# A two-pass list schedule: TensorE's order from a first pass, the other engines ordered by deadlines in a second

## The chip, the core and the metric

The kernel runs on one core of a Trainium2 chip. The metric is the time on the device of one execution, in microseconds (us), as the median of several. The core has five engines with a queue of instructions each: TensorE (PE, the matmuls, with its weight loads shown apart as PEld), VectorE (DVE), ScalarE (ACT), GpSimd (POOL) and SyncE (SP), which here issues the DMA transfers.

## The reference

A trunk of two layers on x of 1024 tokens by 1024 features, all float32. Layer 0 mixes tokens with a gated MLP, layer 1 with an HGRN2 recurrence; each is followed by a gated convolutional feed-forward network. The shifts, scales and gates (`mod`) come from a vector c through a matrix of 1024 by 6144 for each layer.

```python
cond = jax.nn.silu(c)
for i in range(DEPTH):
    mod = (cond @ ada_w[i] + ada_b[i])[:, None, :]
    sh1, sc1, g1, sh2, sc2, g2 = jnp.split(mod, 6, axis=-1)
    h = rms_norm(x, norm_g[i, 0]) * (1.0 + sc1) + sh1
    if i % N_MIXERS == 0:
        y = spatial_gating_mixer(h, ...)   # (gelu(h @ w_u) * (ws @ layernorm(gelu(h @ w_v)) + b)) @ w_out
    else:
        y = hgrn2_mixer(h, ...)            # q, f, i, g = h @ w_in; gated recurrence in chunks of 64; @ w_out
    x = x + g1 * y
    h = rms_norm(x, norm_g[i, 1]) * (1.0 + sc2) + sh2
    x = x + g2 * conv_ffn(h, ...)          # (gelu(conv3(h @ w_gate)) * conv3(h @ w_val)) @ w_down
return rms_norm(x, final_g)
```

## The kernel before

Every float32 matmul is made of three: both operands are split into a high piece (ACT, a copy in a shorter format) and a low piece (the rest, a subtraction on DVE or POOL), and `mm3` (L247) multiplies high by high, high by low and low by high. `p_split` (L442 to L448) makes the two pieces of a weight or of a sum, `p_h` (L428 to L433) those of a normalized activation. Most large products go by a Strassen scheme: a pair of weight blocks gives seven products of sums of quarters. `p_comb` (L455) and `shifted` (L621) make the sums, `snap` (L673, ACT) and `add` (L676, DVE) bring the products out of PSUM.

The stages follow one another in time, by the profile's clock: the start (x arrives, its mean square, first modulations); the v half of the gated MLP, whose result goes to DRAM (`vd`); the u half with the spatial mix (L1194) of v, which is loaded again (L1163) and normalized on ACT (`norm`, L1171), and gated on DVE (`done`, L1210), about 230 to 400 us; the out-projection (`block_out`), 400 to 543, which loads weights (`in_wo`) and gated activations (`gact`) from DRAM; the feed-forward up-projection with its convolution (`conv` L831, `finish` L813), 543 to 1000, and down-projection, to 1220; the HGRN2 scan, to 1710; its out-projection, to 1800; the second feed-forward network, to 2440; and the final norm (`diag` L313, `bcast` L318 on PE, `p_final` L1667).

The modulations are dot products on DVE: `p_ada` loads 512 KB of the matrix (`in_ada`) and `p_dot` or `first_values` multiplies and sums it (`ada_dot`, L255). Those of layer 1 are spread as filler over the stages of layer 0.

What sets the order: the code does not issue instructions as it is written. `Plan.op` records an operation (one or a few instructions) with its engine, a stated duration, what it reads and writes, and a priority `pr` written by hand. `emit` (L162) then runs a list schedule over all operations: on every step it takes, among those that are ready, the one that could start earliest by the stated durations, and among equals the one with the lowest `pr`. Operations of DVE and POOL with `port=True` are never put at the same time. The result is one fixed order for each engine and for SP's queue of DMA issues; the engines then run in that order, each waiting by semaphores for what it needs.

Of the kernel before, what the change touches and what calls it, by code (L numbers as in the profile page):

```python
# [98 lines left out]

class Plan:  # L100
# [9 lines left out]
    LOAD = 2.0  # L110

# [50 lines left out]
    def emit(self):  # L162
        n = len(self.ops)
        left = [0] * n
        users = [[] for _ in range(n)]
        for i, o in enumerate(self.ops):
            for q in set(o[3]):
                users[q].append(i)
                left[i] += 1
# [7 lines left out]
        while len(order) < n:  # L177
            best = None
            for eng, lst in ready.items():
                f = free.get(eng, 0.0)  # L180
                for i in lst:
                    o = self.ops[i]
                    t = max(f, est[i], port if o[5] else 0.0)
                    if best is None or (t, o[4], i) < best:
                        best = (t, o[4], i)
            t, _, i = best
            eng, dur, fn, _, _, pt = self.ops[i]
# [26 lines left out]
def trunk(tc, a, pool, psum, dram):  # L214
# [168 lines left out]
    def p_evac(pl, ps, d, hs, gate, which, pr):  # L383
# [23 lines left out]
    def p_stats(pl, nm, accv, ps, rbv, pr, part=0):  # L407
# [8 lines left out]
        pl.op("V", 1.3, chain, r=(ps,), w=(sm,), pr=pr)  # L416
# [25 lines left out]
    def p_split(pl, src, hi, lo, eng, pr, *preds):  # L442
# [4 lines left out]
        return pl.op(eng, (0.1 + 0.53 * w) if eng == "V" else 0.1 + 1.17 * w,  # L447
# [131 lines left out]
    class Pairs:  # L579
# [32 lines left out]
        def combos(self, k, pr, t1=None):  # L612
# [7 lines left out]
            def shifted(out, x, s, y, srg, pr):  # L620
                pl.op("V", 0.67, lambda: V.scalar_tensor_tensor(out=out.f, in0=x.f, scalar=s, in1=y.f,  # L621
# [26 lines left out]
        def pair(self, j, fine=False):  # L648
# [26 lines left out]
            def add(c, ps, i):  # L675
                pl.op("V", 0.75, lambda: V.tensor_tensor(out=c.f, in0=ps.f, in1=c.f, op=ALU.add), r=(ps, c),  # L676
# [1112 lines left out]
```

## Time and profile before

| | |
|---|---|
| median of 3 runs | 2470.67 us (2470.39 to 2472.54) |
| the profiled execution | 2468.28 us, of which the span of the core's instructions is 2466.5 us |
| TensorE busy | 2419.2 us, 98% of the span |
| VectorE, ScalarE, GpSimd busy | 1992.3, 1205.9, 487.2 us |
| mean granted TensorE clock | 0.993 of full speed |

The span runs from the first to the last instruction; the 1.8 us between it and the execution's time lie around it. A busy share is an average over stages with different limits: a stage is read by its own windows.

### The profile page before, as it was taken

What the parts mean: (1) busy time and instruction counts of PE and PEld (TensorE: products, weight loads), DVE (VectorE), ACT (ScalarE), POOL (GpSimd) and SP (SyncE); (2) the same over time, 40 slices, a digit from 0 to 9 for tenths busy, and PEclk for the clock granted to TensorE, in tenths of its full rate; (3) what the DMA queues carried; (4) which work ended last, traced back from release to release, by engine and by line L of the source; (5) the groups of instructions that cost most, each with busy time, mean ns of one, the idle gap of its engine ahead of it and who ended that gap; (6) DMA issues with size and microseconds to landing.
All of it is one profiled execution on the core that took longest, in us unless ns stands there. A gap on an engine that the chain in (4) does not pass through costs nothing.

```text
span 2466.5 us, 33569 instructions
## 1 busy us (share of the span) xinstructions
PE 2419.2 (98%) x11850; PEld 2024.6 (82%) x11850; DVE 1992.3 (81%) x3179; ACT 1205.9 (49%) x2067; POOL 487.2 (20%) x294
## 2 busy tenths in 40 slices
PE   9999999999999999999999999999999999999997
PEld 7878777788788888888899898888777888888886
DVE  8989987988998888967746666658998998889766
ACT  5324654455555554445544444435454555554544
POOL 0232211122222221013321111100312222220122
PEclk9999999999999999999999999999999999999998
DMA  9997678621333324734110111123302332238332
GB/s 356 305 344 272 200 238 295 222 77 39 116 102 108 116 94 143 262 112 120 51 48 35 58 42 56 44 73 106 106 24 95 98 132 99 94 127 283 95 116 81
DMA packets 156411, 332.00 MB, mean 135 GB/s; under 512 B 15825, under 2 KB 34641, under 8 KB 156242
## 3 DMA queue, kind: packets, MB, share of 16 engines
q1 hardware_dynamic: 156242, 329.86, 40.0%
q8 instruction: 93, 1.52, 0.3%
q14 instruction: 76, 0.62, 0.1%
HBM read 254.82 MB, written 74.97 MB: 134 GB/s over the span
## 4 chain that ended last, share of the span: by engine, by line
PE 76%; DVE 8%; DMA 3%; ACT 2%; issue 1%; SPq 0%; DVEq 0%; ACTq 0%
PE pb L247 69%; PE pb L1462 3%; DMA n<-in_wo 1%; DMA xT<-vd 1%; DMA n<-in_down 1%; DVE h L448 1%; ACT xT L1171 1%; PE pb L1531 1%; PE pb L1551 1%; DVE w L448 1%; DVE raw L831 1%; PE pb L1553 1%; DVE n L448 0%; DVE xT L455 0%; DVE w L455 0%
## 5 line engine op out<-in xcount | busy, mean ns | idle before, releaser
L247 PE MATMUL pb<-h,w 128*128 128x512 f32 (+1 forms) x4212 | 981.7, 389 | 12.8 <-DVE h L448 4.1
L247 PE MATMUL pb<-n,w 128*128 128x512 f32 x3936 | 951.6, 394 | 6.8 <-ACT wk L673 4.4
L247 PEld LDWEIGHTS pb<-h,w 128*128 128x128 f32 x4212 | 785.5, 188 | 185.0 <-DVE h L448 9.6
L247 PEld LDWEIGHTS pb<-n,w 128*128 128x128 f32 x3936 | 731.9, 188 | 160.0 <-ACT wk L673 5.5
L448 POOL TENSOR_TENSOR w<-w,w 128x512 fp32r<-128x512 f32 x158 | 252.2, 1604 | 862.5 <-ACT w L445 784.2
L445 ACT ACTIVATE w<-w 128x512 fp32r<-128x512 f32 x384 | 237.3, 626 | 212.4 <-PE pb L247 121.7
L247 PE MATMUL pb<-w,n 128*128 128x512 f32 (+1 forms) x1536 | 273.6, 338 | 3.0 <-POOL w L448 1.7
L247 PEld LDWEIGHTS pb<-w,n 128*128 128x128 f32 x1536 | 237.9, 190 | 36.3 <-POOL w L448 2.1
L831 DVE SCALAR_TENSOR_TENSOR raw<-wk,prm,raw 128x1024 f32<-128x1024 f32 x168 | 251.7, 1520 | 16.2 <-ACT raw L827 14.1
L448 POOL TENSOR_TENSOR w<-raw,w 128x1024 fp32r<-128x1024 f32 (+1 forms) x48 | 118.3, 2473 | 536.0 <-ACT w L445 467.0
L448 DVE TENSOR_TENSOR w<-w,w 128x512 fp32r<-128x512 f32 x226 | 166.4, 741 | 41.5 <-ACT w L445 41.4
L673 ACT ACTIVATE wk<-pb 128x512 f32<-128x512 f32 x160 | 95.2, 599 | 174.5 <-PE pb L247 161.9
L445 ACT ACTIVATE w<-n 128x512 fp32r<-128x512 f32 x136 | 85.7, 630 | 158.0 <-PE pb L247 143.7
L676 DVE TENSOR_TENSOR wk<-pb,wk 128x512 f32<-128x512 f32 x160 | 109.2, 687 | 50.1 <-PE pb L247 30.9
L448 DVE TENSOR_TENSOR w<-n,w 128x512 fp32r<-128x512 f32 x136 | 103.4, 763 | 56.5 <-ACT w L445 56.4
L445 ACT ACTIVATE h<-h 128x512 fp32r<-128x512 f32 x198 | 122.3, 619 | 40.8 <-DMA h<-gact 23.5
L827 ACT ACTIVATE raw<-wk,prm 128x1024 f32<-128x1024 f32 x84 | 104.2, 1243 | 41.6 <-DVE wk L676 34.9
L448 POOL TENSOR_TENSOR h<-h,h 128x512 fp32r<-128x512 f32 x48 | 67.8, 1413 | 258.8 <-ACT h L445 247.4
L1468 DVE TENSOR_TENSOR wk<-wk 128x256 f32<-128x256 f32 x192 | 95.6, 523 | 23.7 <-PE pb L1462 11.0
L255 DVE SCALAR_TENSOR_TENSOR h<-h,raw 128x1024 f32<-128x1024 f32 x81 | 111.1, 1404 | 3.5 <-DMA h<-in_ada 3.4
L448 DVE TENSOR_TENSOR h<-h,h 128x512 fp32r<-128x512 f32 x150 | 102.1, 686 | 8.7 <-ACT h L445 8.7
L1472 ACT ACTIVATE wk<-wk 128x256 f32<-128x256 f32 x192 | 73.9, 415 | 59.4 <-PE pb L1462 44.2
(217 smaller groups left out, 2431.8 us busy)
## 6 DMA issues: line engine op xcount, KB each, us to landing
w<-in_up SPq DMA_DIRECT2D x88, 512.0 KB, 3.5
h<-in_ada SPq DMA_DIRECT2D x81, 512.0 KB, 6.3
act<-raw SPq DMA_DIRECT2D x154, 256.0 KB, 2.0
h<-act SPq DMA_DIRECT2D x124, 256.0 KB, 2.7
n<-in_down SPq DMA_DIRECT2D x64, 256.0 KB, 5.3
h<-gact SPq DMA_DIRECT2D x56, 256.0 KB, 2.7
gact<-xT SPq DMA_DIRECT2D x52, 256.0 KB, 3.9
vd<-h SPq DMA_DIRECT2D x32, 256.0 KB, 5.1
```

The lines of the kernel that those rows point to most:

```text
L247: PE.matmul(ps, L[i // 2], R[i % 2], start=first and i == 0 and not more, stop=last and i == 2, skip_group_check=more)
L255: V.scalar_tensor_tensor(out=raw, in0=raw, scalar=1.0, in1=condr, op0=ALU.mult, op1=ALU.mult, accum_out=mod[:, m:m + 1])
L445: pl.op("S", 0.2 + 0.43 * w, lambda: S.activation(hi.r, src.f, AF.Copy), r=(src,), w=(hi,), pr=pr)
L448: lambda: e.tensor_tensor(out=lo.r, in0=src.f, in1=hi.f, op=ALU.subtract), *preds,
L673: pl.op("S", 0.6, lambda: S.activation(c.f, ps.f, AF.Copy), r=(ps,), w=(c,), pr=p(i) - 10)
L676: pl.op("V", 0.75, lambda: V.tensor_tensor(out=c.f, in0=ps.f, in1=c.f, op=ALU.add), r=(ps, c), w=(c,), pr=p(i) - 8)
L827: pl.op("S", 1.15, lambda: S.activation(y.f, wk[:, o + PADW:o + PADW + T], AF.Identity, bias=pc("conv_b", l * NUP + b), scale=cw(2)), r=(c ...
L831: pl.op("V", 1.17, lambda w=w: V.scalar_tensor_tensor(out=y.f, in0=wk[:, o + w:o + w + T], scalar=cw(w), in1=y.f, op0=ALU.mult, op1=ALU.ad ...
L1171: S.activation(x, x, AF.Identity, scale=lnr[:, tb:tb + 1], bias=nmr[:, tb:tb + 1])
L1462: PE.matmul(ps_()[0:m, c, :], K.f[:, c * P:c * P + m], q, start=True, stop=True)
L1468: V.tensor_tensor(out=halves_(X2, s)[:, :, i, :], in0=halves_(X, s)[:, :, i, :], in1=pair2()[:, :, o].unsqueeze(2).to_broadcast([P, 256 // ...
L1472: S.activation(halves_(X2, s)[:, :, i, :], halves_(X, s)[:, :, i, :], AF.Copy)
```

## The change

`emit` schedules twice. The first pass is the old schedule by hand priorities. From it comes PE's order. Each PE operation then gets as its due time the sum of the stated durations of the PE operations ahead of it; an operation of another engine gets the earliest due time of what uses its result, less its own stated duration and a lag, and one whose result nothing on PE uses gets the end of the plan. The second pass is the same list schedule (earliest start first), with PE's operations ranked by their place in the first order and the others by due time, in place of `pr`. Beside that the stated durations of some operations are set to what was measured. No instruction is added, taken away or altered; the orders on the engines and the order of SP's DMA issues differ.

```diff
-    def emit(self):
+    def lag(self, i, u):
+        eng, e2 = self.ops[i][0], self.ops[u][0]
+        return self.LOAD if eng == "D" else self.LAT if e2 != eng else self.CHAIN if eng == "V" else 0.0
+
+    def schedule(self, users, rank):
...
                 for i in lst:
-                    o = self.ops[i]
-                    t = max(f, est[i], port if o[5] else 0.0)
-                    if best is None or (t, o[4], i) < best:
-                        best = (t, o[4], i)
+                    t = max(f, est[i], port if self.ops[i][5] else 0.0)
+                    if best is None or (t, rank[i], i) < best:
+                        best = (t, rank[i], i)
...
+    def emit(self):
...
+        order = self.schedule(users, [o[4] for o in self.ops])
+        for _ in range(self.ROUNDS):
+            on_pe = [i for i in order if self.ops[i][0] == "PE"]
+            late, t = [FAR] * n, 0.0
+            for i in on_pe:
+                late[i] = t
+                t += self.ops[i][1]
+            for i in reversed(order):
+                for u in users[i]:
+                    late[i] = min(late[i], late[u] - self.lag(i, u) - self.ops[i][1])
+            rank = [min(x, t) for x in late]
+            for k, i in enumerate(on_pe):
+                rank[i] = k
+            order = self.schedule(users, rank)
+        for i in order:
             self.ops[i][2]()
...
-        pl.op("V", 1.3, chain, r=(ps,), w=(sm,), pr=pr)
+        pl.op("V", 1.95, chain, r=(ps,), w=(sm,), pr=pr)
...
-        return pl.op(eng, (0.1 + 0.53 * w) if eng == "V" else 0.1 + 1.17 * w,
+        return pl.op(eng, (0.11 + 0.57 * w) if eng == "V" else 0.1 + 1.22 * w,
...
-                    pl.op("S", 1.2, norm, r=(v, kv(3280 + 4 * hf, 4), kv(3544 + 4 * hf, 4)), w=(v,), pr=pr - 3)
+                    pl.op("S", 1.6, norm, r=(v, kv(3280 + 4 * hf, 4), kv(3544 + 4 * hf, 4)), w=(v,), pr=pr - 3)
```

Three places in the orders. A row is the line, the operation, and out<-in by the program's names; lines of the changed kernel stand 25 higher from `trunk_body` on (L255 is L280 there, L433 L458, L448 L473, L459 L484).

**DVE at the start**, about 19 to 27 us: the row at L433 (L458), `n100`, is the low piece of the first activation block; the five rows from L255 to L970 (L280 to L995) behind or ahead of it are `first_values` of the second block, and `w1`, `w3` are low pieces of weights. Before:

```order
L448 TENSOR_TENSOR w1_196<-h2_133,w0_167 128x1024
L448 TENSOR_TENSOR w3_202<-h3_145,w2_176 128x1024
L433 SCALAR_TENSOR_TENSOR n100_207<-h11_186,mod_70,n000_200 128x512
L255 SCALAR_TENSOR_TENSOR h4_162,mod_70<-h4_162,raw2_67 128x1024
L255 SCALAR_TENSOR_TENSOR h5_172,mod_70<-h5_172,raw2_67 128x1024
L263 TENSOR_TENSOR mod_70<-mod_70,prm_63 128x2
L267 SCALAR_TENSOR_TENSOR amul_71<-mod_70,prm_63 128x1
L970 SCALAR_TENSOR_TENSOR h11_186<-xT_64,amul_71,h10_198 128x512
L448 TENSOR_TENSOR w5_244<-h6_179,w4_205 128x1024
```

And of the change:

```order
L995 SCALAR_TENSOR_TENSOR h11_186<-xT_64,amul_71,pb6_81 128x512
L473 TENSOR_TENSOR w3_198<-h3_132,w2_164 128x1024
L473 TENSOR_TENSOR w1_203<-h2_140,w0_174 128x1024
L280 SCALAR_TENSOR_TENSOR h4_160,mod_70<-h4_160,raw2_67 128x1024
L280 SCALAR_TENSOR_TENSOR h5_170,mod_70<-h5_170,raw2_67 128x1024
L288 TENSOR_TENSOR mod_70<-mod_70,prm_63 128x2
L292 SCALAR_TENSOR_TENSOR amul_71<-mod_70,prm_63 128x1
L995 SCALAR_TENSOR_TENSOR h11_186<-xT_64,amul_71,h10_205 128x512
L458 SCALAR_TENSOR_TENSOR n100_207<-h11_186,mod_70,n000_201 128x512
```

The low piece `n100` went from ahead of the second block's five rows to behind them.

**SP's queue of DMA issues**, where the gated MLP's out-projection loads stand (`n...<-in_wo` are weights, `h11` and `h2<-gact` activations, `in_ada` modulations of layer 1, `gact<-xT` stores). Before:

```order
L459 DMA n021_2973<-in_wo 128x512
L459 DMA h11_2988<-gact_84 128x512
L459 DMA h2_2993<-gact_84 128x512
L459 DMA n031_2996<-in_wo 128x512
L459 DMA raw1_66<-in_ada 128x1024
L739 DMA gact_84<-xT_64 128x512
L459 DMA h11_2988<-gact_84 128x512
L459 DMA h2_2993<-gact_84 128x512
L459 DMA h11_2988<-gact_84 128x512
L459 DMA h10_3038<-in_ada 128x1024
L459 DMA n101_3051<-in_wo 128x512
L739 DMA gact_84<-xT_64 128x512 x4
```

And of the change:

```order
L484 DMA n021_2972<-in_wo 128x512
L484 DMA h11_2988<-gact_84 128x512
L484 DMA h2_2993<-gact_84 128x512
L484 DMA n031_2997<-in_wo 128x512
L484 DMA n101_3000<-in_wo 128x512
L484 DMA h11_2988<-gact_84 128x512
L484 DMA h2_2993<-gact_84 128x512
L484 DMA n111_3025<-in_wo 128x512
L484 DMA n121_3029<-in_wo 128x512
L484 DMA h11_2988<-gact_84 128x512
L484 DMA n131_3046<-in_wo 128x512
L484 DMA h2_2993<-gact_84 128x512
```

Two loads of modulations stood here among those of the out-projection; in the change its next loads have their places. From the load of `n001` to that of `n071` eight stood in the queue before, and none stands there in the change.

**DVE ahead of the HGRN2 out-projection's fifth product**, about 1731 to 1738 us: `n041`, `n141` and so on are the low pieces for it (L448, L473), `raw2`, `h0`, `h9` and `n020` to `n130` are sums for later (L455, L480), `xT` an evacuation (L387, L412). Before:

```order
L1575 SCALAR_TENSOR_TENSOR h9_9709<-pb2_77,prm_63,h6_8816 128x512
L455 TENSOR_TENSOR n120_12939<-n060_12844,n020_12841 128x512
L455 TENSOR_TENSOR raw2_67<-h9_9709,raw2_67 128x512
L455 TENSOR_TENSOR h0_9273<-h9_9709,h0_9273 128x512
L455 TENSOR_TENSOR h9_9709<-h9_9709,raw2_67 128x512
L455 TENSOR_TENSOR n030_12882<-w8_12158,n030_12882 128x512
L448 TENSOR_TENSOR n041_12712<-n100_12833,n001_12650 128x512
L387 SCALAR_TENSOR_TENSOR xT_64<-pb0_75,mod_70,xT_64 128x512
L387 SCALAR_TENSOR_TENSOR xT_64<-pb1_76,mod_70,xT_64 128x512
L455 TENSOR_TENSOR n130_12979<-n070_12888,n030_12882 128x512
L448 TENSOR_TENSOR n141_12769<-w1_12161,n101_12669 128x512
```

And of the change:

```order
L1600 SCALAR_TENSOR_TENSOR h9_9710<-pb2_77,prm_63,h6_8845 128x512
L473 TENSOR_TENSOR n041_12675<-n100_12894,n001_12633 128x512
L473 TENSOR_TENSOR n141_12682<-w1_12158,n101_12635 128x512
L480 TENSOR_TENSOR raw2_67<-h9_9710,raw2_67 128x512
L473 TENSOR_TENSOR n051_12751<-n110_12896,n011_12644 128x512
L473 TENSOR_TENSOR n151_12793<-w1_12158,n111_12648 128x512
L480 TENSOR_TENSOR n020_12790<-w8_12160,n020_12790 128x512
L473 TENSOR_TENSOR n161_12842<-w5_12211,n121_12663 128x512
```

The low pieces `n041` and `n141` come right behind `h9`, ahead of the sums that stood in front of them.

## Rows read from the trace of the kernel before

**Rows 1.** The profile page: busy time of the engines (us, share of the span, instructions).

```profile
PE 2419.2 (98%) x11850; PEld 2024.6 (82%) x11850; DVE 1992.3 (81%) x3179; ACT 1205.9 (49%) x2067; POOL 487.2 (20%) x294
```

**Rows 2.** Windows by stage: us of the stretch, busy us (and instructions) of PE, PEld, DVE, ACT, POOL, then TensorE's granted clock as a share of full speed, the DMA share and GB/s.

```profile
100.00:200.00 100.00, 98.33 (x430) 80.06 (x429) 89.48 (x142) 27.36 (x43) 35.56 (x14) 1.00 0.91 322
...
620.00:700.00 80.00, 78.84 (x344) 64.44 (x345) 76.66 (x87) 42.68 (x61) 22.23 (x12) 1.00 0.33 112
700.00:900.00 200.00, 200.00 (x884) 165.67 (x883) 178.38 (x209) 103.76 (x148) 43.32 (x31) 1.00 0.32 110
...
1220.00:1700.00 480.00, 479.06 (x3157) 429.58 (x3156) 295.48 (x744) 207.76 (x442) 71.41 (x32) 1.00 0.15 50
```

**Rows 3.** Finer windows, same columns.

```profile
260.00:280.00 20.00, 16.87 (x77) 13.86 (x76) 20.00 (x31) 14.88 (x34) 6.83 (x2) 0.91 0.58 191
...
400.00:420.00 20.00, 17.63 (x69) 13.59 (x68) 13.90 (x22) 8.72 (x15) 1.29 (x1) 0.91 0.98 342
420.00:440.00 20.00, 18.07 (x79) 14.26 (x78) 16.95 (x28) 7.75 (x13) 0.00 (x0) 1.00 0.94 333
440.00:460.00 20.00, 18.99 (x82) 14.77 (x81) 18.46 (x32) 10.49 (x19) 0.00 (x0) 1.00 0.94 336
...
1840.00:1860.00 20.00, 18.38 (x75) 13.50 (x74) 19.84 (x28) 10.88 (x19) 5.08 (x3) 1.00 0.04 14
1860.00:1880.00 20.00, 16.22 (x62) 12.87 (x61) 15.10 (x14) 9.27 (x14) 5.67 (x4) 0.86 0.27 92
```

**Rows 4.** What PE waited for over the whole span, from the chain of waits: us in total, times, longest us.

```profile
PE pb L318 <- DVE h L313: 7.7, 6, 4.9
PE pb L247 <- ACT xT L673: 4.6, 4, 1.6
...
PE pb L247 <- POOL w L448: 1.7, 1, 1.7
```

**Rows 5.** Timeline of PE and of DVE at the start: start us, us, engine, line, operation, out<-in, count; in brackets the idle time before it and what ended it.

```profile
21.39 5.75 PE L247 MATMUL pb<-w,n 128*128 128x512 f32 x24 [0.93 <-ACT n L432]
27.31 0.98 PE L247 MATMUL pb<-w,n 128*128 128x512 f32 x3 [0.17 <-ACT n L432]
...
22.28 0.75 DVE L433 SCALAR_TENSOR_TENSOR n<-h,mod,n 128x512 fp32r<-128x512 f32 x1
22.94 1.22 DVE L255 SCALAR_TENSOR_TENSOR h<-h,raw 128x1024 f32<-128x1024 f32 x1
...
25.75 0.75 DVE L970 SCALAR_TENSOR_TENSOR h<-xT,amul,h 128x512 f32<-128x512 f32 x1
```

**Rows 6.** Timeline of PE and of ACT in the u half: the spatial mix that waits, and a product whose bank ACT frees.

```profile
263.01 1.74 PE L1194 MATMUL pb<-wk,xT 128*128 128x128 f32 x8 [2.43 <-ACT h L445]
...
369.35 0.96 PE L247 MATMUL pb<-h,w 128*128 128x512 f32 x3 [1.57 <-ACT xT L673]
...
367.17 1.65 ACT L1171 ACTIVATE xT<-xT,wk 128x128 f32<-128x128 f32 x4 [0.32 <-DMA xT<-vd]
368.72 0.57 ACT L673 ACTIVATE xT<-pb 128x512 f32<-128x512 f32 x1
```

**Rows 7.** Issues of loads from 366 to 441 us by L459: count, then the issuing instruction's own ns min/median/max, first and last start; and PE's waits in that stretch.

```profile
L459 SPq DMA_DIRECT2D h<-in_ada x6: 327/327/463, 403.6 to 440.7; - x6
L459 SPq DMA_DIRECT2D raw<-in_ada x5: 328/333/377, 366.7 to 419.4; - x5
...
402.53 0.50 PE L247 MATMUL pb<-h,w 128*128 128x512 f32 x1 [2.06 <-ACT h L445]
...
432.02 2.83 PE L247 MATMUL pb<-h,w 128*128 128x512 f32 x11 [1.78 <-DVE w L448]
```

**Rows 8.** DMA issues by kind: count, KB each, median us from issue to landing.

```profile
h<-in_ada SPq DMA_DIRECT2D x81, 512.0 KB, 6.3
```

**Rows 9.** Timeline of PE and of DVE around two waits for a low piece.

```profile
620.10 0.74 PE L247 MATMUL pb<-h,w 128*128 128x512 f32 x2 [1.13 <-DVE h L448]
...
1738.93 2.37 PE L247 MATMUL pb<-n,n 128*128 128x512 f32 x9 [2.90 <-DVE n L448]
...
1737.11 1.76 DVE L448 TENSOR_TENSOR n<-w,n 128x512 fp32r<-128x512 f32 x1
1738.80 0.68 DVE L448 TENSOR_TENSOR n<-n,n 128x512 fp32r<-128x512 f32 x1
```

**Rows 10.** Timeline of PE and of DVE at the second feed-forward network's entry; and DVE's `finish` steps over the whole span (busy us, mean ns of one, idle before).

```profile
1875.08 8.64 PE L247 MATMUL pb<-n,w 128*128 128x512 f32 x24 [3.78 <-ACT wk L673]
...
1870.36 2.30 DVE L831 SCALAR_TENSOR_TENSOR wk<-wk,prm 128x1024 f32<-128x1024 f32 x1
...
1873.18 1.21 DVE L813 TENSOR_TENSOR raw<-raw,wk 128x1024 f32<-128x1024 f32 x1
...
L813 DVE TENSOR_TENSOR raw<-raw,raw 128x1024 f32<-128x1024 f32 x40 | 53.5, 1337 | 1.7
```

**Rows 11.** Timeline of the tail.

```profile
2448.38 0.16 DVE L289 TENSOR_TENSOR small<-small 128x2 f32<-128x2 f32 x1
...
2450.85 5.75 POOL L1667 TENSOR_TENSOR xT<-xT,h 128x256 f32<-128x256 f32 x8 [17.26 <-ACT h L322]
...
2454.61 0.65 DVE L285 TENSOR_TENSOR small<-small 128x2 f32<-128x2 f32 x1
...
2457.92 1.22 PE L318 MATMUL pb<-h,ones 128*128 128x256 f32 x2 [4.91 <-DVE h L313]
```

More of the change, by code (lines that the diff above doesn't have):

```diff
@@ L97, in r @@
         return self.life.ap()[:, self.o:self.o + self.n]
+FAR = 1e9
 class Plan:
@@ L110 @@
     LOAD = 2.0
+    ROUNDS = 1
     def __init__(self):
@@ L160, in op @@
         return i
-    def emit(self):
+    def lag(self, i, u):
+        eng, e2 = self.ops[i][0], self.ops[u][0]
+        return self.LOAD if eng == "D" else self.LAT if e2 != eng else self.CHAIN if eng == "V" else 0.0
+    def schedule(self, users, rank):
         n = len(self.ops)
[L164 to L169, printed above, removed]
+        left = [len(o[3]) for o in self.ops]
         est, end = [0.0] * n, [0.0] * n
@@ L194, in emit @@
             for u in users[i]:
-                e2 = self.ops[u][0]
-                lat = self.LOAD if eng == "D" else self.LAT if e2 != eng else self.CHAIN if eng == "V" else 0.0
-                est[u] = max(est[u], end[i] + lat)
+                est[u] = max(est[u], end[i] + self.lag(i, u))
                 left[u] -= 1
                 if not left[u]:
-                    ready.setdefault(e2, []).append(u)
-        for _, _, i in sorted(order):
+                    ready.setdefault(self.ops[u][0], []).append(u)
+        return [i for _, _, i in sorted(order)]
+    def emit(self):
+        n = len(self.ops)
+        users = [[] for _ in range(n)]
+        for i, o in enumerate(self.ops):
+            for q in o[3]:
+                users[q].append(i)
+        order = self.schedule(users, [o[4] for o in self.ops])
[13 more added lines that the diff above has]
+        for i in order:
             self.ops[i][2]()
-        return max(end)
 def trunk_body(tc, a):
@@ L388, in fn @@
                                    op0=ALU.mult, op1=ALU.add)
-        return pl.op("V", 0.15 + 0.6 * w, fn, r=(ps, x, modrg(*which, d)), w=(x,), pr=pr)
+        return pl.op("V", 0.13 + 0.56 * w, fn, r=(ps, x, modrg(*which, d)), w=(x,), pr=pr)
     def p_sum(pl, nm, d, accv, sqs, pr, eng="V", first=0):
@@ L422, in p_t @@
         i = (l * 2 + sub) * KT + d
-        return pl.op("V", 0.67, lambda: V.scalar_tensor_tensor(out=tv.f, in0=xT[:, d, nm.hs],
+        return pl.op("V", 0.69, lambda: V.scalar_tensor_tensor(out=tv.f, in0=xT[:, d, nm.hs],
                                                                scalar=amul[:, i:i + 1], in1=nm.rb,
@@ L620, in shifted @@
             def shifted(out, x, s, y, srg, pr):
-                pl.op("V", 0.67, lambda: V.scalar_tensor_tensor(out=out.f, in0=x.f, scalar=s, in1=y.f,
+                pl.op("V", 0.69, lambda: V.scalar_tensor_tensor(out=out.f, in0=x.f, scalar=s, in1=y.f,
                                                                 op0=ALU.add, op1=ALU.subtract),
@@ L675, in add @@
             def add(c, ps, i):
-                pl.op("V", 0.75, lambda: V.tensor_tensor(out=c.f, in0=ps.f, in1=c.f, op=ALU.add), r=(ps, c),
+                pl.op("V", 0.69, lambda: V.tensor_tensor(out=c.f, in0=ps.f, in1=c.f, op=ALU.add), r=(ps, c),
                       w=(c,), pr=p(i) - 8)
@@ L812, in finish @@
             yg, yv = ys
-            pl.op("V", 1.15, lambda: V.tensor_tensor(out=yg.f, in0=yg.f, in1=yv.f, op=ALU.mult), r=(yg, yv),
+            pl.op("V", 1.21, lambda: V.tensor_tensor(out=yg.f, in0=yg.f, in1=yv.f, op=ALU.mult), r=(yg, yv),
                   w=(yg,), pr=pr - 1, port=True)
@@ L826, in conv @@
             crg = ("wk", o, o + PADW + T)
-            pl.op("S", 1.15, lambda: S.activation(y.f, wk[:, o + PADW:o + PADW + T], AF.Identity,
+            pl.op("S", 1.22, lambda: S.activation(y.f, wk[:, o + PADW:o + PADW + T], AF.Identity,
                                                   bias=pc("conv_b", l * NUP + b), scale=cw(2)),
@@ L1209, in done @@
                 pl.op("S", 0.62, lambda: S.activation(u.f, u.f, AF.Gelu), r=(u,), w=(u,), pr=pr)
-            pl.op("V", 0.75, lambda: V.tensor_tensor(out=u.f, in0=ps.f, in1=u.f, op=ALU.mult), r=(ps, u), w=(u,), pr=pr,
+            pl.op("V", 0.69, lambda: V.tensor_tensor(out=u.f, in0=ps.f, in1=u.f, op=ALU.mult), r=(ps, u), w=(u,), pr=pr,
                   port=False)
@@ L1406, in project @@
             f, kk = fs.next(), k1
-            op("S", 0.65, lambda: S.activation(f.f, s_.f, AF.Identity, scale=omc[:, h:h + 1], bias=lbc[:, h:h + 1]),
+            op("S", 0.79, lambda: S.activation(f.f, s_.f, AF.Identity, scale=omc[:, h:h + 1], bias=lbc[:, h:h + 1]),
                (s_,), (f,))
```

26 lines of the change are left out of this document (13 added, 13 removed).

## The prediction

> **What bounds the kernel now.** I read the page first, then windows over the whole span, then PE's waits, and at the end the timelines around them. The page says that PE is busy 98% of the span [rows 1], so an order that only moves work can win no more than the rest, 47.3 us, and what half clock costs beside it. The windows say where that rest is. In the steady part of the first feed-forward network PE is busy 200.00 of 200 us, with 884 matmuls, or 200/884 = 0.226 us for one of full width; the scan has 479.06 of 480 [rows 2]. Nothing can be won there, only lost. The holes lie at 100 to 200 us (1.67 us idle), 620 to 700 (1.16) [rows 2], and in the short windows [rows 3]: 260 to 280 has 3.13 us idle and a granted clock of 0.91; 400 to 460 has 69 + 79 + 82 = 230 matmuls, 52.0 us of steady work, so 8.0 us are lost; 1840 to 1880 has 75 + 62 = 137, 31.0 us of work, so 9.0 us are lost. [...] The waits name the rest: DVE's low piece at 1739 us (2.90) [rows 9], ACT's snaps in the u half (4.6 in four waits), the final norm (7.7), a POOL piece (1.7) [rows 4].
>
> These holes are of three kinds. In one, DVE is full (20.00 of 20 us at 260, 19.84 at 1840) and the piece that PE wants stands behind work that nobody wants yet. In the second, at 400 to 460, the DMA share is 0.94 to 0.98 [rows 3]: the bytes bound the stage. The third is the tail, a chain of dependent steps. The change can do something for the first two.
>
> **The change, part by part.** No instruction comes or goes; I cost moves alone, and how many operations stand ahead of a piece is counted in the two orders. The sum is made against the profiled execution, 2468.28 us; the median of the runs is 2.4 us above it, and I add that at the end. A difference under 0.2% (4.9 us) can hardly be told from none.
>
> *Start.* On DVE the low piece `n100` of the first block now stands behind the five `first_values` rows of the second. Before, it ran at 22.28 and took 0.75 us; the five took from 22.94 to 25.75 + 0.75 [rows 5]. PE's order is the same there: 24 matmuls from 21.39 on, eight high by high and then those that need `n100`. Eight at 0.226 last until 23.2. With `n100` behind, it comes 26.50 - 22.94 = 3.6 us later, at 26.6, and may save the 0.5 us by which a condition product (c by its sigmoid) now stands behind the mean square's sums. So PE stops for about 3 us, and the 16 matmuls that are left end at 30 in place of 27.1. The next block's pieces come no sooner than before, by at most 0.75 us, and PE waited only 0.17 us for them [rows 5]: little slack gives the loss back. I take **-2.5**; bounds +0.5 (the condition product's gain alone) and -5 (3.2, and 1.8 as at 260 if the clock falls). [...] The two rows, 22.28 then 22.94, show order kept but cannot tell whether it must be.
>
> *100 to 200 us.* One wait of 1.7 us for a POOL piece [rows 4]; DVE has fewer modulation dots ahead of it. I take +1 of the 1.67, bounds 0 and 1.7.
>
> *260 to 300 us.* PE's mix waited 2.43 us [rows 6], with the clock 3.13 + 1.8 = 4.9 us lost. The gating product that frees its bank has 16 DVE operations fewer ahead of it in the new order. At the 0.65 us that one took in the full window (20.00/31) [rows 3] that is 10 us. DVE is full, though, so what is passed over is due a little later. +3.5; bounds 0 and 4.9.
>
> *300 to 370 us.* Four snaps stand on ACT behind `norm`, which waits for v's load: at 369 the norm took 367.17 to 368.72, the snap came then, and PE had waited 1.57 us [rows 6]. On ACT the order of the two is nearly the same; what changes is that fewer modulation loads share the DMA, and the loads of v have earlier places. +2 of the 4.6, bounds 0 and 4.6.
>
> *400 to 460 us.* This is the largest term. Before, 11 modulation loads of 512 KB were issued between 366.7 and 440.7 [rows 7, 8]; the eight among the out-projection's loads go behind them. At 337 GB/s (mean of the three windows [rows 3]) 8 x 0.524 MB = 4.2 MB are 12.4 us of DMA time, in a stretch that lost 8.0 us for bytes. The first of its waits, 2.06 us at 402.53 [rows 7], also hangs on an activation that is stored and read back and cannot be asked for sooner, so not all comes back: **+5.5**, bounds 2 and 8. The dots themselves cost DVE the same later, from 460 on, where PE's window of the next feed-forward stage shows DVE with room (178.38 of 200 [rows 2]).
>
> *620 us.* The wait of 1.13 us [rows 9] is for a low piece that has 9 DVE operations fewer ahead: +1.2 with its neighbours, bounds 0 and 1.2 (all the idle time of that window).
>
> *1739 us.* PE waited 2.90 us for a low piece, 1.76 us long, from 1737.11 [rows 9]. `n041` and `n141` now come 6 to 8 rows sooner, more than the wait: **+2.9**, bounds 1 and 2.9. [...] 1.76 us in place of the 0.68 us of its neighbours is 1.08 us more, while POOL ran. [...]
>
> *1840 to 1880 us.* 9.0 us are lost here. The low pieces that PE wanted at 1852 to 1860 stand 4 to 6 operations sooner, at 0.71 us each (19.84/28 [rows 3]) 2.8 to 4.3 us. But the long wait, 3.78 us at 1875, is for a bank that a tap of the convolution (2.30 us) and a `finish` (1.21) have to free [rows 10], and these move by 2 operations alone on a full DVE; what PE gains in front it then waits here. +3; bounds 0 and 9.0.
>
> *Elsewhere.* PE's own order differs by 159 of 2359 operations, within the feed-forward stages, where PE waits for nothing; 0, with the bounds in the rivals. The tail keeps its chain: the small steps cost 0.65 us beside POOL's final products and 0.16 alone [rows 11], and the new order starts those products about 1 us later, which moves more of them onto the chain: -0.5, bounds -2 and +1.
>
> Sum: -2.5 + 1 + 3.5 + 2 + 5.5 + 1.2 + 2.9 + 3 - 0.5 = 16.1 us. Profiled 2468.28 - 16.1 = 2452.2; as a median 2454.6, say **2454**.
>
> **Rivals.** *The waits only move.* Where DVE is full, an earlier piece makes another late; the gains at 100, 260, 620 and 1840 go, and those by fewer bytes (5.5), half of those in the u half (1) and at 1739 (2.9) stay: 9.4 - 2.5 - 0.5 = 6.4, so 2464. For it: 20.00 and 19.84 of 20. Against: both are short; the windows behind them have room. 0.2.
>
> *Nearly all waits go.* Every upper bound with the start as taken: 1.7 + 4.9 + 4.6 + 8 + 1.2 + 2.9 + 9 + 1 - 2.5 = 30.8, so 2440. Against: two full stretches on DVE. 0.09.
>
> *Slower.* DVE takes its work in order, and due times push `finish` steps back until a split that PE wants stands right behind one: in the new order the `finish` of the first feed-forward pair has moved 29 operations back, among the splits of the next pair. There are 40 such steps, 1.34 us each [rows 10]. If half of them hold PE up for their whole length, 20 x 1.34 = 26.8 us go: 2470.67 - 16.1 + 26.8 = 2481. From 16.1/1.34 = 12 of them on the gain is gone, from 16 on the kernel is slower by 4.9 us. Against: DVE has 10% room in the steady part [rows 2] and the splits run ahead of PE there. 0.13.
>
> *No change.* The moved instructions do not matter, or the start's loss and half a dozen new small waits take what is won: within 4.9 us of 2470.67. PE at 98% speaks for it. 0.13.
>
> **How the numbers follow.** My forecast holds 0.45. Its own range, with the bounds of the largest terms taken half way, is 2447 to 2462. Faster by over 0.2%: 0.45 + 0.09 + most of the first rival (0.17) = 0.71; within 0.2%: 0.13 and the rest of it, 0.16; slower: 0.13. The range for 8 in 10 leaves out the slow rival and a little beside, and the end of the fast one: 2439 to 2472.
>
> **What the profile of the changed kernel would show.** At the start PE's row of 24 matmuls from 21.4 is cut after eight by an idle of about 3 us. At 400 to 460 the matmuls rise from 230 to about 255 and no load of modulations is issued between those of the out-projection; the waits by the low piece at 1739 and by the mix at 263 are gone or under 1 us; at 1875 a wait of 2 us or more stays. The steady windows keep 200.00 busy. I am wrong if one of these has new idle time on PE ended by a DVE low piece or an ACT snap, if DMA at 400 to 460 is as full as before with as many waits, or if the wait at 1875 grows with half clock behind it.

## The result

| | before | changed |
|---|---|---|
| median, us | 2470.53 (2466.74 to 2472.54, 4 runs) | 2454.02 (2451.04 to 2458.03, 4 runs) |
| ratio to before, 95% interval | | 0.9944 (0.993 to 0.9958) |
| span of the profiled execution, us | 2466.5 | 2454.1 |

The change made the kernel faster by 0.42 to 0.70%, which is 10 to 17 us. The forecast was 2454. In the two profiled executions the difference is 12.4 us, where the sum said 16.1: the total came out well, in part by luck, since several of its terms did not.

The page's first line, to hold against [rows 1]: PE is busy 2.7 us less, and the span is 12.4 us shorter, so PE's idle time fell by 9.7 us, from 47.3 to 37.6.

```profile
PE 2416.5 (98%) x11850; PEld 2026.7 (83%) x11850; DVE 1991.1 (81%) x3179; ACT 1200.6 (49%) x2067; POOL 478.3 (19%) x294
```

Windows of the changed kernel, columns as in [rows 2, 3]; the first two and that at 1730 have no counterpart there.

```profile
0.00:20.00 20.00, 18.03 (x79) 15.23 (x80) 11.29 (x28) 11.31 (x15) 0.20 (x4) 0.74 0.94 354
20.00:40.00 20.00, 16.39 (x64) 13.13 (x64) 18.25 (x31) 7.41 (x9) 0.00 (x0) 0.83 0.98 351
...
100.00:200.00 100.00, 100.00 (x443) 82.78 (x442) 82.32 (x137) 30.61 (x46) 31.71 (x14) 1.00 0.87 308
...
260.00:280.00 20.00, 19.13 (x93) 14.78 (x92) 19.67 (x31) 15.03 (x35) 2.58 (x2) 1.00 0.61 196
...
400.00:420.00 20.00, 19.55 (x87) 15.85 (x86) 18.07 (x28) 10.50 (x18) 0.91 (x1) 1.00 0.96 342
420.00:440.00 20.00, 20.00 (x90) 16.57 (x89) 19.36 (x32) 8.08 (x14) 0.00 (x0) 1.00 1.03 369
440.00:460.00 20.00, 20.00 (x90) 16.57 (x89) 18.50 (x31) 9.50 (x17) 1.51 (x1) 1.00 0.92 310
...
700.00:900.00 200.00, 200.00 (x884) 165.59 (x883) 178.97 (x205) 103.22 (x149) 49.58 (x31) 1.00 0.34 111
...
1730.00:1740.00 10.00, 7.90 (x28) 6.04 (x28) 8.32 (x14) 4.97 (x9) 4.93 (x3) 0.83 0.36 116
...
1840.00:1860.00 20.00, 17.09 (x59) 12.48 (x58) 19.05 (x25) 10.06 (x14) 3.17 (x2) 0.83 0.13 41
1860.00:1880.00 20.00, 18.97 (x84) 15.38 (x83) 16.30 (x24) 8.87 (x14) 3.81 (x3) 1.00 0.49 158
```

The out-projection is full now: 87 + 90 + 90 = 267 matmuls where 230 ran [rows 3]. The DMA share there is 0.96, 1.03 and 0.92, much as before: what PE gained is not an emptier DMA. The steady window has the same 884. Ahead of the final norm the granted clock is 0.83 or less at three places, all with an idle PE: the start (0.74 and 0.83), 1730 (0.83), and 1840 (0.83). In finer windows it is 0.50 throughout from 10 to 18, 26 to 32, 1736 to 1739 and 1849 to 1855 us: that is the half clock of this text.

PE's longest waits, against [rows 4]. The POOL piece at 164 us is gone, the snaps L698 (L673) of `xT` fell from 4.6 to 1.2 us; that for the low piece of an activation, L458 (L433), grew from 0.9 to 4.3. The last row is of the kernel before.

```profile
PE pb L343 <- DVE h L338: 7.3, 2, 5.7
PE pb L272 <- DVE n L473: 4.9, 5, 2.1
PE pb L272 <- DVE n L458: 4.3, 2, 3.6
...
PE pb L272 <- ACT xT L698: 1.2, 2, 0.9
...
PE pb L247 <- DVE n L433: 0.9, 2, 0.7
```

To see each stage's share I took the end of the same PE operation in both traces, at places where both orders have the same operations behind them, and subtracted. The difference grows by the stage's gain:

| from before's | forecast, us | measured, us |
|---|---|---|
| start to 43 us | -2.5 | -5.1 |
| to 165 us | +1 | +2.2 |
| to 308 us (the mix at 263) | +3.5 | +2.1 |
| to 372 us (snaps of the u half) | +2 | +3.1 |
| to 457 us (out-projection) | +5.5 | +7.9 |
| to 693 us | +1.2 | +1.2 |
| to 1572 us (feed-forward, scan) | 0 | +0.4 |
| to 1806 us (the piece at 1739) | +2.9 | +0.6 |
| to 1884 us | +3 | -0.3 |
| to the end | -0.5 | +0.3 |
| sum | 16.1 | 12.4 |

These are the stages of one execution of each kernel. Three of the experiments below have the changed kernel's orders but for their own edit (the start's inversion undone, four dots left out, GpSimd's sums left out), and the same measure taken from their traces tells what belongs to the order. To 165 us it is +2.2 in all, the out-projection +7.2 to +8.3. But the stage to 693 us, +1.2 above, is -1.5, -4.8 and -0.5 there; that to 1806, +0.6 above, is +2.1, +2.1 and +3.2; that to 1884, -0.3 above, is +1.5, +1.5 and +1.1.

### The profile page after: what moved, and what is told of

It reads as the page before. It is cut to its first block, busy times and chain, and to the rows that moved or that the text cites. A ratio compares the mean times of both kernels' runs of the same rounds, so it can differ in the third digit from the quotient of the medians.

```text
span 2454.1 us, 33489 instructions
## 1 busy us (share of the span) xinstructions
PE 2416.5 (98%) x11850; PEld 2026.7 (83%) x11850; DVE 1991.1 (81%) x3179; ACT 1200.6 (49%) x2067; POOL 478.3 (19%) x294
## 3 DMA queue, kind: packets, MB, share of 16 engines
q8 instruction: 93, 1.52, 0.3%
## 4 chain that ended last, share of the span: by engine, by line
PE 94%; DVE 4%; DMA 2%; ACT 1%; issue 0%; SPq 0%; DVEq 0%; ACTq 0%
PE pb L272 86%; PE pb L1487 4%; PE pb L1219 1%; DVE h L473 1%; PE pb L1556 1%; PE pb L1576 1%; PE pb L1578 0%; DMA h<-act 0%; PE pb L343 0%; DVE n L473 0%; PE pb L1549 0%; PE pb L1598 0%; DVE h L280 0%; DMA w<-in_wu 0%; PE pb L333 0%
## 5 line engine op out<-in xcount | busy, mean ns | idle before, releaser
L473 POOL TENSOR_TENSOR w<-w,w 128x512 fp32r<-128x512 f32 x158 | 249.1, 1583 | 861.9 <-ACT w L470 762.1
L856 DVE SCALAR_TENSOR_TENSOR raw<-wk,prm,raw 128x1024 f32<-128x1024 f32 x168 | 267.6, 1603 | 5.5 <-ACT raw L852 4.2
L473 POOL TENSOR_TENSOR w<-raw,w 128x1024 fp32r<-128x1024 f32 (+1 forms) x48 | 115.5, 2417 | 532.4 <-ACT w L470 420.4
L473 DVE TENSOR_TENSOR w<-w,w 128x512 fp32r<-128x512 f32 x226 | 161.2, 718 | 38.0 <-ACT w L470 37.0
L698 ACT ACTIVATE wk<-pb 128x512 f32<-128x512 f32 x160 | 94.7, 594 | 136.6 <-PE pb L272 114.9
L473 DVE TENSOR_TENSOR w<-n,w 128x512 fp32r<-128x512 f32 x136 | 101.9, 752 | 61.8 <-ACT w L470 61.5
L470 ACT ACTIVATE h<-h 128x512 fp32r<-128x512 f32 x198 | 122.0, 617 | 16.1 <-DVE h L473 5.8
L473 POOL TENSOR_TENSOR h<-h,h 128x512 fp32r<-128x512 f32 x48 | 68.7, 1432 | 253.5 <-ACT h L470 246.7
L473 DVE TENSOR_TENSOR h<-h,h 128x512 fp32r<-128x512 f32 x150 | 109.4, 732 | 4.4 <-ACT h L470 4.4
L280 DVE SCALAR_TENSOR_TENSOR h<-h,raw 128x1024 f32<-128x1024 f32 x81 | 102.6, 1293 | 1.4 <-DMA h<-in_ada 1.3
```

The lines of the kernel that those rows point to most:

```text
L280: V.scalar_tensor_tensor(out=raw, in0=raw, scalar=1.0, in1=condr, op0=ALU.mult, op1=ALU.mult, accum_out=mod[:, m:m + 1])
L470: pl.op("S", 0.2 + 0.43 * w, lambda: S.activation(hi.r, src.f, AF.Copy), r=(src,), w=(hi,), pr=pr)
L473: lambda: e.tensor_tensor(out=lo.r, in0=src.f, in1=hi.f, op=ALU.subtract), *preds,
L698: pl.op("S", 0.6, lambda: S.activation(c.f, ps.f, AF.Copy), r=(ps,), w=(c,), pr=p(i) - 10)
L856: pl.op("V", 1.26, lambda w=w: V.scalar_tensor_tensor(out=y.f, in0=wk[:, o + w:o + w + T], scalar=cw(w), in1=y.f, op0=ALU.mult, op1=ALU.ad ...
```

## The experiments

Each is told with its median and its ratio to the kernel before on the same chip; before's median was 2468.86, 2469.35 and 2469.27 us in the three series. The changed kernel was timed in another, where before stood at 2470.53, so a difference of medians to it is uncertain by 1.2 to 1.7 us beside the spread of the runs.

**The start's inversion.** A helper merges the engines' lists after one operation is moved in its list.

```diff
+    FIRST = (71, 81)     # n100's low piece, first_values of the second block
...
-        for i in order:
+        for i in self.merge(users, order, *self.FIRST):
             self.ops[i][2]()
...
+        lane.remove(x)
+        lane.insert(lane.index(y), x)
```

> The changed kernel with one operation put back: on VectorE the low piece n100 of the first activation block ahead of the five first_values rows of the second; every other order is kept. Theory (that inversion makes the whole loss of 5.6 us at the start: an idle of 3.61 us and then half clock): TensorE's 24 matmuls run unbroken from 21 us on, no half clock behind them, and the time is 5 to 6 us under the changed kernel, about 2448.5. Rival (the start is bound by its loads, DMA 0.98 there, and the wait turns up again at the next block): under 1.5 us of gain, 2452.5 or more.

2447.89 us, ratio 0.991 (0.9895 to 0.9925): 6.1 us under the changed kernel. Timelines of PE at the start, first of the changed kernel, then of the experiment (its lines stand 20 higher again):

```profile
20.82 2.11 PE L272 MATMUL pb<-w,n 128*128 128x512 f32 x8
26.54 7.79 PE L272 MATMUL pb<-w,n 128*128 128x512 f32 x21 [3.61 <-DVE n L458]
```

```profile
20.15 6.14 PE L292 MATMUL pb<-w,n 128*128 128x512 f32 x24
26.63 5.73 PE L292 MATMUL pb<-w,n 128*128 128x512 f32 x24 [0.34 <-ACT n L477]
...
20.00:40.00 20.00, 19.11 (x81) 14.67 (x81) 19.61 (x33) 6.78 (x9) 0.00 (x0) 1.00 0.98 365
```

The row of 24 is cut after eight in the changed kernel, as forecast, and 21 matmuls behind it take 7.79 us, or 0.37 each in place of 0.226. It is whole in the experiment, with the clock at 1.00. The inversion makes the loss, and half clock a good part of it. In the measure of the stage table the start comes to +0.5 where the changed kernel has -5.1.

**The two halves of the change.** The new stated durations with the old single pass, and the two passes with the old durations:

```diff
-    ROUNDS = 1
+    ROUNDS = 0
```

> The changed kernel with ROUNDS = 0: the new stated durations with the old single pass by hand priorities. Nine loads of modulations stand again between the out-projection's n001 and n071, and n100 stands ahead. Theory (the due times of the second pass make the gain): 400 to 460 us has 230 to 238 matmuls as before, and the time is 2466 to 2472. Rival (the durations alone make it): 2458 or less.

2485.34 us, ratio 1.0061 (1.0048 to 1.0073): slower than before by 12 to 18 us, with 241 matmuls at 400 to 460 us. Neither side had expected a loss. The time goes into waits all over the later stages: PE's idle time is 5.75 us at 620 to 700, 8.23 at 1820 to 1900 and 3.28 at 1900 to 2220, where before had 1.16, 5.40 and none. The first of these windows, against that of [rows 2]:

```profile
620.00:700.00 80.00, 74.25 (x318) 60.06 (x316) 69.72 (x79) 39.91 (x58) 18.57 (x12) 0.98 0.29 99
```

> The two passes with the stated durations of before. n100 stands behind the five rows, no load of modulations stands between n001 and n071. Theory (due times, not durations): loss at the start about 5 us, 400 to 460 us has 255 to 265 matmuls, the time is 2451 to 2459. Rival (a due time is worth no more than the durations it is made of): 2463 or more.

2452.51 us, ratio 0.9934 (0.9921 to 0.9946): no different from the whole change (0.9944). Its start loses 3.1 us, and 400 to 460 us has 260 matmuls. So the second pass makes all of the gain; the durations alone do harm, and under due times they do nothing that can be measured.

**One number of the kernel before**, which puts the last modulations behind the out-projection's loads by hand:

```diff
-    p_ada(Seq(rv(1), whole(hc[0], F32)), len(ada_todo), OB0 + 4)
+    p_ada(Seq(rv(1), whole(hc[0], F32)), len(ada_todo), OB0 + 30)
```

> The kernel before with one number changed: the hand priority of the last group of modulations OB0 + 30 in place of OB0 + 4, so that their loads and dots stand behind the out-projection's loads. Theory (the bytes of eight modulations bind 400 to 460 us): 255 to 265 matmuls there in place of 230, 5.5 to 8 us gained, 2462.5 to 2465. Rival (what counts there is VectorE's order of the low pieces): 230 to 240 matmuls, 2468.5 or more.

2464.55 us, ratio 0.9984 (0.9975 to 0.9992): 2 to 6 us. Its windows:

```profile
400.00:420.00 20.00, 16.69 (x72) 12.90 (x71) 13.27 (x20) 9.74 (x17) 3.88 (x3) 1.00 0.98 339
420.00:440.00 20.00, 20.00 (x90) 16.57 (x89) 14.75 (x24) 9.02 (x16) 0.00 (x0) 1.00 0.97 343
440.00:460.00 20.00, 20.00 (x90) 16.57 (x89) 20.00 (x34) 9.24 (x16) 0.00 (x0) 1.00 0.74 272
```

252 matmuls, 22 more than before, or 5.0 us: all that was lost from 420 us on is back, and the first 20 us are as empty as they were. That is a little less than the 255 matmuls and 5.5 us of the theory.

**Their loads left out of the kernel before**, the dots kept:

```diff
+            if m in (76, 78, 88, 90, 92, 93, 94, 95):
...
+                pl.ops[-2] = (*o[:2], lambda: None, *o[3:])     # no load; the dot multiplies another tile
```

> The kernel before; left out are the loads of the eight modulations that stood among the out-projection's; their dots keep place and length but multiply another tile, so eight modulation blocks are wrong; all orders stay. Theory (the bytes bind 400 to 460 us): at least the 5.0 us that moving them behind gave back there (252 matmuls against 230), so 250 to 262 matmuls. Rival (the dots on VectorE were in the way): under 238 matmuls.

2464.81 us, ratio 0.998 (0.9971 to 0.999).

```profile
400.00:420.00 20.00, 16.86 (x65) 13.24 (x66) 13.90 (x22) 8.18 (x14) 1.28 (x1) 0.91 0.77 264
420.00:440.00 20.00, 19.65 (x87) 15.94 (x86) 19.29 (x33) 9.16 (x15) 0.00 (x0) 1.00 0.82 267
440.00:460.00 20.00, 20.00 (x90) 16.57 (x89) 19.94 (x35) 11.99 (x21) 0.00 (x0) 1.00 0.82 286
```

242 matmuls, between the two expectations. From 420 us on there are 177 where before had 161: that is what these loads cost there, since every dot is still in its place. That it is their bytes is not shown, because two other things left with them: the dots' waits for their data (1.9 us on DVE in this stretch), and the loads' places in SP's queue. Before, that queue stood still for 10.4 us between 400 and 460 us, since a load of modulations is issued when a dot has read the tile that it overwrites, and loads of the out-projection stood behind it. SP's waits in the kernel before, of 400 to 460 us:

```profile
SPq L459 <- DVE h L255: 10.4, 4, 3.2
```

From 400 to 420 nothing is won: one wait for the first activation stays (3.6 us, 2.06 before), with half clock behind it (0.91 granted over these 20 us, 13 matmuls in 5.09). The loads are about half of this term; the first wait is another matter.

**The same loads put back in the changed kernel:**

```diff
+            for i in self.soon:        # loads and dots of the last group of modulations
+                rank[i] = 0.0
             order = self.schedule(users, rank)
```

> The changed kernel with one part undone: the last group of modulations, loads and dots, gets the earliest due time in place of the latest, so that eight of its loads stand again between the out-projection's n001 and n071. Theory (their place is what made the largest gain): 400 to 460 us falls from 263 matmuls to 230 to 250, and 4 to 8 us of the gain go, 2458 to 2462. Rival (the out-projection's own loads, asked for sooner, made it): 255 matmuls or more, the time within 1.5 us of the changed kernel.

2459.56 us, ratio 0.9962 (0.995 to 0.9974): 5.5 us of the gain are gone, and 400 to 460 us has 250 matmuls. (The changed kernel has 267 there and not the 263 of the expectation.) Timeline of PE, then of DVE and of SP ahead of it (lines of the helpers stand 3 higher), and the longest of SP's waits at 380 to 403 us:

```profile
401.51 8.75 PE L275 MATMUL pb<-h,w 128*128 128x512 f32 x26 [5.52 <-ACT h L473]
...
388.46 1.23 DVE L283 SCALAR_TENSOR_TENSOR raw<-raw,raw 128x1024 f32<-128x1024 f32 x1 [2.76 <-DMA raw<-in_ada]
...
394.57 0.33 SPq L487 DMA_DIRECT2D raw<-in_ada  x1
394.99 0.86 SPq L487 DMA_DIRECT2D h<-gact  x2
...
SPq L487 <- DVE raw L283: 8.2, 4, 3.1
```

There it is a different wait from the one that I had priced. DVE stands still for 2.76 us because the dot at the head of its queue has no data, and the next dots come late. SP's queue stands with them, 8.2 us in four waits: a load of modulations is issued when a dot has read its tile (394.57), and the load of the first activation stands right behind it (394.99; the changed kernel issues that load at 391.73). The last store ahead of that load had been issued by 386.1, so the store is not what came late. PE waits 5.52 us once. From 420 on this kernel runs full (90 and 90 matmuls), with the modulations' bytes in the stage, a DMA share of 0.95 and 0.96, and 9.9 us of SP's waits for dots from 400 to 460: neither the bytes nor a queue that stands makes the loss from 420 on by itself. A dot in the wrong place costs twice: what stands behind it on DVE (2.76 us here), and what stands behind its load in SP's queue (8.2).

**The dots at 259 to 275 us left out of the changed kernel:**

```diff
+            if m in (67, 69, 81, 83):
...
+                pl.ops[-1] = (*o[:2], lambda m=m: V.memset(mod[:, m:m + 1], 0.0), *o[3:])
```

> The changed kernel; left out are four modulation dots that VectorE ran between 259 and 275 us (1.2 us each, a short memset in their place, so four modulation blocks are zero); all orders stay. In the changed kernel TensorE lost 3.7 us between 264 and 287 us. Theory (VectorE is full there and dots that nobody on TensorE wants stand ahead of its pieces): TensorE's idle time at 260 to 300 us falls from 2.69 to under 1 us, and 1.5 to 3.5 us are gained. Rival (the pieces are late for another reason): over 2 us idle stay, under 0.7 us gained.

2453.61 us, ratio 0.9932 (0.9918 to 0.9946), 0.4 us under the changed kernel by the medians: the rival's case. Two windows, first of the changed kernel, then of the experiment:

```profile
260.00:300.00 40.00, 37.31 (x186) 29.59 (x185) 37.15 (x59) 27.51 (x62) 6.46 (x5) 1.00 0.64 207
```

```profile
260.00:300.00 40.00, 37.37 (x186) 30.00 (x185) 33.01 (x54) 28.69 (x63) 6.44 (x5) 1.00 0.66 210
```

DVE has 4.1 us less to do, and PE runs the same 186 matmuls with the same idle time. A full DVE was not the reason there. What is, I cannot say: the waits changed their names (a gating product of 1.5 us went, a snap of 1.1 and a low piece of 0.9 came), which looks like a chain through ACT and PE, but no run shows it.

**GpSimd's sums of squares left out of the changed kernel**, for the wait at 1734.8 us:

```diff
+            if eng != "V" and pr > 300:
...
+                pl.ops[-1] = (*o[:2], lambda: None, *o[3:])
```

> The changed kernel; left out are GpSimd's three sums of squares at the entry of the second feed-forward network (so its mean square lacks three blocks); all orders stay. In the changed kernel TensorE waited 2.10 us at 1734.8 for a low piece that took 1.75 us while GpSimd ran, and half clock followed. Theory (the step was lengthened by the GpSimd step beside it): it takes 0.68 us, the wait falls to about 1.0 us, no half clock follows, 1 to 3.5 us are gained. Rival (ScalarE's high piece or the order on VectorE sets that wait): the wait stays over 1.8 us and the time within 0.7 us of the changed kernel.

2452.01 us, ratio 0.9931 (0.9916 to 0.9946); 2 us less than the changed kernel, which runs of this spread cannot tell from nothing. The rows can. Timelines of PE, DVE and POOL, first of the changed kernel, then of the experiment:

```profile
1734.81 7.57 PE L272 MATMUL pb<-n,n 128*128 128x512 f32 x25 [2.10 <-DVE n L473]
...
1733.01 1.75 DVE L473 TENSOR_TENSOR n<-w,n 128x512 fp32r<-128x512 f32 x1
...
1732.49 1.71 POOL L429 TENSOR_TENSOR h<-h,raw 128x512 f32<-128x512 f32 x1
```

```profile
1733.93 8.45 PE L272 MATMUL pb<-n,n 128*128 128x512 f32 x36 [1.06 <-DVE n L476]
...
1733.20 0.68 DVE L476 TENSOR_TENSOR n<-w,n 128x512 fp32r<-128x512 f32 x1
```

Without the GpSimd step beside it the low piece takes 0.68 us, the wait falls from 2.10 to 1.06, and 36 matmuls take 8.45 us (0.235 each) where 25 took 7.57 (0.30): no half clock (1.00 granted over 1730 to 1740, 0.83 in the changed kernel). The wait is shown to hang on that step; the clock is not. With the dots left out the same wait comes at 1739.87, 2.16 us long, and the clock stays up all the same. PE's timeline and a window of that trace:

```profile
1739.87 6.43 PE L272 MATMUL pb<-n,n 128*128 128x512 f32 x27 [2.16 <-DVE n L473]
...
1735.00:1745.00 10.00, 7.84 (x34) 6.14 (x34) 9.76 (x15) 4.99 (x9) 6.21 (x4) 1.00 0.34 113
```

**Two more versions.** The old durations with the start mended (both edits above together):

> Two passes with the stated durations of before and the low piece n100 put ahead of the five first_values rows. Theory (the start's inversion and the rest add up): 5 to 6 us under the 2452.5 of the two passes with old durations, 2446.5 to 2447.5. Rival (what is won at the start is waited for later): 2450 or more.

2450.82 us, ratio 0.9924 (0.9912 to 0.9936): 1.7 us under the two passes alone, where 5 to 6 were expected; runs of this spread exclude neither. The start gains 3.7 us (from -3.1 to +0.6 in the measure of the stage table), and part of it is given back in this execution: PE's idle time at 30 to 100 us rose from 1.03 to 2.53 and at 460 to 620 from 3.50 to 5.45 us, the latter with a wait of 4.2 us for an evacuation:

```profile
PE pb L292 <- DVE xT L432: 4.6, 3, 4.2
```

The same wait is 2.24 us in the two passes alone, 2.59, 3.03 and 1.51 us in the three traces with the changed kernel's orders, and absent in the changed kernel's own. So it is not shown to come from mending the start; why the evacuation is late was not tried. A third pass on top of the mended start:

```diff
-    ROUNDS = 1
+    ROUNDS = 2
```

> The changed kernel with n100 put ahead, as in the first experiment, and a third pass (ROUNDS = 2), whose due times come from the second pass's order. Theory (the first due times hold already what PE's order can tell): within 3 us of that experiment's 2447.9. Rival (due times still improve): 2444 or less.

2449.88 us, ratio 0.9924 (0.9911 to 0.9937): no gain by a further pass. The changed kernel with the start mended, 2447.89 us, has the lowest median of all; its interval overlaps those of these two.

## Why the prediction was right, and where not

The main line held: PE's holes came from pieces and loads that stood behind work nobody wanted yet, and ordering by due time filled part of them, 9.7 us of 47.3. The steady stages gave and took nothing (884 matmuls in the same window). The out-projection is the largest gain, and the start loses, both as forecast. The sum, 16.1, lies inside the measured 10 to 17 us, but partly by luck, because its errors have both signs:

- *Start*, -2.5 said, -5.1 measured, just past the end of the bounds. The idle was sized well (about 3 us said, 3.61 measured). I put half clock into the bound alone; it came (0.50 from 26 to 32 us), and costs about 2.3 us (16 matmuls at 0.37 in place of 0.226). The first experiment gives all of it back. The 1.8 us of clock in this bound and in that of 260 us is an estimate from [rows 3], 20 us times the 0.09 that 0.91 lacks; no run shows it as time lost, but by 1 us the trace of before grants 0.68, 0.50, 0.50 and 0.62 from 263 to 267, which is 1.7 us short of full.
- *400 to 460 us*, +5.5 said, +7.9 measured. The step that failed is that the first activation "cannot be asked for sooner": its load was issued at 391.73 in place of 395.39. Of these 3.7 us the kernel had 2.3 in hand at 372; the rest fits SP's queue, where before loads of x stood ahead of this one and waited 3.6 us for stores to land, and in the changed kernel stand elsewhere. From 400 to 420 us PE ran 87 matmuls in place of 69, and part of that is the half clock that followed the wait before (0.91 [rows 3], 0.50 from 404 to 406). The rest lies from 420 on, where leaving the loads out of the old kernel gave 3.6 us (177 matmuls against 161). That the bytes bind the stage, as I had it, is not shown: the changed kernel runs full with the same DMA share, and so does the one with the loads put back, from 420 on. What in those loads held PE before stays open. Timeline of SP before, its wait at 380 to 403 us, and the same load in the changed kernel:

```profile
395.39 1.26 SPq L459 DMA_DIRECT2D h<-gact  x2
...
SPq L1260 <- DMA gact<-xT: 3.6, 2, 2.2
...
391.73 0.86 SPq L484 DMA_DIRECT2D h<-gact  x2
```

- *620 us*, +1.2 said and measured, by luck. The low piece's wait is gone, but two for a bank came (0.84 and 1.03 us), and the other traces with these orders lose 0.5 to 4.8 us in this stage, with the wait of 1.5 to 3.0 us for an evacuation that is told above.
- *1739 us*, +2.9 said, +0.6 measured. The wait that I priced is gone. Another came 36 matmuls on, 2.10 us at 1734.8, for a low piece that met a GpSimd step. The prediction had the like of it from one row of before, 1.08 us more [rows 9] beside a POOL sum of 1.60 us from 1736.73, and the sum has nothing for it. In the changed kernel's trace the piece ends 0.56 us after the GpSimd step's end (1734.76 and 1734.20), and is 1.07 us shorter without it. Half clock behind that wait (0.50 from 1736 to 1739) cost some 1.6 us more (25 matmuls in 7.57 us, against 0.238 for one in the row at 1739.87), and that belongs to this execution: the other traces have +2.1 and more.
- *1840 to 1880 us*, +3 said, -0.3 measured. The bank's wait at 1875, 3.78 us [rows 10], of which I expected 2 us or more to stay, became one of 1.03. But PE waits elsewhere in the stage: 1.52 us for a high piece at its entry, which had no wait before, 0.73 for the low piece behind that, 1.39 and 0.90 for low pieces at 1847. All waits of the stage come to 6.0 us, where before had 5.8: they moved. Half clock moved with them (0.83 over 1840 to 1860 and 1.00 over 1860 to 1880, where before had 1.00 and 0.86 [rows 3]; by 1 us it is 0.50 from 1849 to 1855 in place of 1875 to 1881); I had counted it as a loss to win back, not as one that can move. The other traces have these waits too, and +1.1 to +1.5; with the start mended the clock is 1.00 over 1820 to 1900, where the changed kernel has 0.96. Timeline of PE there:

```profile
1807.48 0.51 PE L272 MATMUL pb<-n,w 128*128 128x512 f32 x1 [1.52 <-ACT n L457]
...
1847.05 0.96 PE L272 MATMUL pb<-n,w 128*128 128x512 f32 x3 [1.39 <-DVE n L473]
1848.91 1.22 PE L272 MATMUL pb<-n,w 128*128 128x512 f32 x2 [0.90 <-DVE n L473]
1849.93 6.72 PE L272 MATMUL pb<-h,w 128*128 128x512 f32 x18
...
1865.86 6.43 PE L272 MATMUL pb<-n,w 128*128 128x512 f32 x27 [1.03 <-ACT wk L698]
```

- *260 to 300 us*, +3.5 said, +2.1 measured, with a wrong reason for the rest: DVE was not what held PE there.
- *100 to 200* (+2.2 for +1) and *300 to 372* (+3.1 for +2) were taken too low; the wait for POOL is gone outright (100.00 of 100 us busy).
- *Tail*: as forecast, the small steps still run beside GpSimd's products (0.64 to 0.65 us each for six of them up to 2444.6, 0.16 behind them), and the wait grew from 4.91 [rows 11] to 5.7 us; the stage as a whole measured +0.3 where -0.5 was said.

The rival that the waits only move is half true: they moved at 1739 and at 1840. At 1739 that was not because DVE is full (8.32 of 10 us busy); at 1840 it still is nearly so (19.05 of 20). The slow rival's mechanism, a `finish` that holds up a split, is not to be seen. Three waits of 0.84 to 1.03 us are for a bank that a snap frees, but at 1865.86 the snap stood on ACT behind a split that had itself waited for PE (the two rows below), when the `finish` ahead of it had ended at 1862.88. The steady windows have no such wait.

```profile
1864.69 0.63 ACT L470 ACTIVATE w<-w 128x512 fp32r<-128x512 f32 x1 [2.28 <-PE pb L272]
1865.23 0.58 ACT L698 ACTIVATE wk<-pb 128x512 f32<-128x512 f32 x1
```

## What to carry to other kernels

Order an engine by when the bound engine needs the result, and let filler have the latest due time: a filler step costs its own time and the wait of everything behind it, on DVE when its data is late (2.76 us with the loads put back) and in SP's queue when its load waits for a tile that is still read (8.2 us in four waits there). A stated duration is not better for being measured where hand priorities have grown around the old ones: change the rule and the numbers apart, and time both. Take a stage's gain from more than one execution before a cause is put to it. After reordering, look first for inversions of a few steps where the bound engine has no slack (the start, the seam between two stages); one swap there was worth more than a third of the whole change.

## What was not expected of the hardware

Half clock moves with the waits, and not by their length alone. The wait at 1734.8 us stands at the same place in the changed kernel (2.10 us), with the start mended (2.15) and with the dots left out (2.16). In the first, half clock followed (0.83 granted over 1730 to 1740); in the other two the clock is 1.00 (over 1700 to 1820, and over 1735 to 1745), as it is with the wait of 1.06 us (1.00 over 1730 to 1740). The 2.90 us at 1739 in the kernel before [rows 9] had none behind it (1.00 over 1735 to 1745), and a wait of 2.89 us there, with the loads left out, had (0.83 over 1730 to 1740). So two executions of one order can differ by the half clock behind one wait, some 1.6 us here, and one trace does not show that a shorter wait saved it.

Where a step of DVE and one of POOL met at 1733 us, both took longer: the DVE piece 1.75 us in place of 0.68, and POOL's sum, which takes 1.28 us in the row below, where no such piece runs, 1.71:

```profile
1736.28 1.28 POOL L429 TENSOR_TENSOR h<-h,raw 128x512 f32<-128x512 f32 x1 [2.08 <-ACT raw L424]
```
